# Seven half-size products for one pair of up tiles: a block of the Strassen kind in the MLP of an encoder trunk

## The chip, the cores and the metric

The kernel runs on one core of one Trainium2 chip. The time is the device time of one execution in microseconds. Three runs of the kernel before took 1680.46 to 1681.95 us, the median is 1681.14 us.

The core's engines work side by side and meet through semaphores: TensorE (PE in the profile, PEld for its weight loads) multiplies matrices and writes into PSUM, VectorE (DVE) and ScalarE (ACT) do elementwise work, GpSimd (POOL) and SyncE (SP) here mostly issue DMA transfers.

## The reference: what is computed

Two layers on 512 tokens of width 1024. Each layer has a token part (attention and retention branches, merged and normalised) and a channel part, which is where the change lies:

```python
def conv_glu_ffn(x, w_up, conv_w, conv_b, w_down):
    h = x @ w_up                                    # 512 x 1024 by 1024 x 5632
    hp = jnp.pad(h, ((0, 0), (1, 1), (0, 0)))
    h = hp[:, :-2] * conv_w[0] + hp[:, 1:-1] * conv_w[1] + hp[:, 2:] * conv_w[2] + conv_b
    a, b = jnp.split(h, 2, axis=-1)
    return (jax.nn.gelu(a) * b) @ w_down            # 2816 x 1024
...
ple = jax.nn.sigmoid(x @ w_ple_gate[i]) * (p[i] @ w_ple_proj[i])
x = layer_norm(DEEPNORM_ALPHA * x + ffn + ple, ln2_g[i], ln2_b[i])
```

The convolution runs along the tokens, with a width of three, on each of the 5632 up channels by itself. Everything is float32.

## The kernel before

**Products of split numbers.** Each float32 operand is split into a high part and a low part (`split`, line 169: ACT copies the high part, DVE subtracts to get the low part), and a product is three matmuls, high by high, high by low and low by high (`mm3`, line 395). An instruction name `hi<-raw` in the profile is ACT's cast of a weight, `lo<-raw` is DVE's subtraction for the same weight.

**Weights as a stream.** `Stream` (line 275) holds all weights of the whole program as a list of items in the order in which the products take them. `load` issues the DMA of an item on SP's queue, `prep` splits it into its two halves, and `get` hands it to a product; each `get` first prepares some items ahead (at most `deep`, 5) and loads three more. Plain weights go through a pool of three raw buffers and three pairs of halves (`N_RAW`, `N_W`). For a Strassen-like product, weights are sums of blocks of the matrix: `block_items` (line 187) makes the seven items a, c, t1, t2, d, t3 and t4, where t1, t2 and t4 come from a's raw buffer by adding one more block after another, each by an accumulating DMA on POOL's queue (`add`), and t3 from a second buffer. These two raw buffers (`rawa`, `rawt`) belong to the pool `up`, and so do the halves of the items that are listed as held.

**The pool of units.** `up` is a pool of 30 units (`N_UNIT`, line 29) of 4 KB in each partition. The tiles that live long are taken from it: R, xn, the operands of the down products, sums of x, held weights, own raw buffers. A tile takes a free unit when it is first written and gives it back after its last reader. If none is free, the writing instruction waits.

**Order.** In the MLP the order of the instructions on each of the five queues is pinned to the program's order (`_Ordered.on = set(ORD)`). An instruction that waits holds up all that stands behind it on its engine.

**The MLP's stages.** After the first layer norm, x1 stands transposed in `xt`. The stages are:

- the PLE gate (`pg`, line 1340): seven products of the Strassen kind on halves of x1, with 512 columns each, and between them five plain up tiles. `vg_sums` (line 673) makes the sums of x1 that four of the products take: S, eight units, two for each of t1, t2, d and t3. Behind products c, d, t3 and t4, `ple_gate` multiplies the gate into R and adds xn to it, which frees xn.
- three segments (`SEGS`, line 36) of 3, 4 and 4 pairs of up tiles. Segment 0 has one up tile left beside the five that stand in `pg`. An up tile (`up_tile`, line 1266) is two GEMMs `gemm_t` of 24 matmuls of 128x512, one for each half of the gated unit. ACT scales the middle tap out of PSUM (`ca<-gt,cw`), DVE adds the two side taps, ACT applies GELU to the first half and DVE multiplies. `up_step` (line 1299) splits the result into an operand of the down products: the first tile of a pair gives `a11` (half a unit), the second gives `k2`, and `s_parts` forms the sums `sa` and `sb` of the pair.
- behind each segment, the down products a, c, t1, t2, d, t3 and t4, with 128x512 matmuls over the segment's pairs. N1 halves accumulate in four PSUM banks over all three segments (`w`, `x4`), so the banks that remain are four. In segment 0 the halves of both a's and c's weights are held in units (`HELD[3]`), in segments 1 and 2 those of c's alone. The sums of the last pair are formed after product a.

The matmuls of 128x256 that the change uses exist elsewhere already: `product_t` (line 1078) does the half-size products of the gate blocks in the token part, seven for a block, each with 24 matmuls and x or sums of x as the moving operand.

## Time and profile before

| what | value |
|---|---|
| median of three runs | 1681.14 us (1680.46 to 1681.95) |
| the profiled execution: span from the first to the last instruction | 1679.3 us |
| its own time beside the span | not given by the page; the runs' median is 1.8 us above the span |
| PE busy | 1669.5 us, 99% of the span |
| DVE busy | 1228.2 us, 73% |
| ACT busy | 949.1 us, 57% |
| POOL busy | 189.2 us, 11% |
| DMA | 289.68 MB, mean 172 GB/s |
| granted TensorE clock | 0.999 of full speed |

The profile is of one execution. A group is named by line, engine, operation and the program's tile names, written as out<-in. Most of the MLP's instructions bear line 90, the helper through which the pinned instructions go, so they are told apart by their tiles. The chain of waits is followed back from the last instruction to what released it. A busy PE is not a PE at its peak: matmuls overlap, and what a matmul costs is read from the distance of starts.

### The profile page before, as it was taken

How to read it: one execution, taken by the hardware profiler on the slowest of the kernel's cores; microseconds unless marked ns; L12 is line 12 of the kernel's file. 1: busy time of each engine (PE TensorE's matmuls, PEld its weight loads, DVE VectorE, ACT ScalarE, POOL GpSimd, SP SyncE). 2: the span in 40 equal slices, each digit the busy share in tenths (PEclk: the TensorE clock that was granted, in tenths of full speed). 3: DMA queues.
4: the chain of work that ended last, by engine and by line, in shares of the span. 5: the costliest groups of instructions: out<-in, count | busy, mean ns of one | idle time of the engine just before them, and what ended most of it. 6: DMA issues, size and time to landing. Idle time of an engine off the chain costs nothing.

```text
span 1679.3 us, 22089 instructions
## 1 busy us (share of the span) xinstructions
PE 1669.5 (99%) x8325; PEld 1418.1 (84%) x8325; DVE 1228.2 (73%) x1857; ACT 949.1 (57%) x1418; POOL 189.2 (11%) x216
## 2 busy tenths in 40 slices
PE   9999999999999999999999999999999999999997
PEld 7889988888888888888888899888888888888886
DVE  6756676776787767757876566877688887676678
ACT  6765676853366535335476647668534574353354
POOL 1111111110200100100112011111002010000003
PEclk9999999999999999999999999999999999999999
DMA  8989666666655535535788795667667565265274
GB/s 303 249 234 233 171 149 139 165 173 223 207 135 161 121 112 163 135 111 172 193 231 219 184 245 163 138 144 170 160 241 225 130 171 126 88 181 132 89 212 101
DMA packets 87530, 289.68 MB, mean 172 GB/s; under 512 B 9984, under 2 KB 14592, under 8 KB 87424
## 3 DMA queue, kind: packets, MB, share of 16 engines
q1 hardware_dynamic: 62512, 199.66, 33.7%
q0 software_dynamic: 24912, 88.62, 30.2%
q8 instruction: 65, 1.06, 0.3%
q14 instruction: 41, 0.34, 0.1%
HBM read 269.36 MB, written 17.30 MB: 171 GB/s over the span
## 4 chain that ended last, share of the span: by engine, by line
PE 99%; DVE 1%; ACT 0%; POOL 0%; issue 0%; DVEq 0%; POOLq 0%; ACTq 0%
PE gt L90 31%; PE u L90 13%; PE v L90 7%; PE gt L397 6%; PE gt L398 6%; PE gt L399 6%; PE w L90 4%; PE gn L399 3%; PE gn L397 3%; PE gn L398 3%; PE x L90 1%; PE u L397 1%; PE u L399 1%; PE u L398 1%; PE gn L90 1%; PE na L1023 1%
## 5 line engine op out<-in xcount | busy, mean ns | idle before, releaser
L90 PE MATMUL gt<-x1t,hi 128*128 128x512 f32 x1408 | 433.5, 389 | 0.0
L90 PEld LDWEIGHTS gt<-x1t,hi 128*128 128x128 f32 x1408 | 264.3, 188 | 55.0
L90 PE MATMUL gt<-x1t,lo 128*128 128x512 f32 x704 | 274.1, 389 | 0.1
L90 DVE TENSOR_TENSOR lo<-raw,hi 128x1024 fp32r<-128x1024 f32 (+1 forms) x147 | 175.9, 1206 | 43.5 <-ACT hi L90 43.3
L90 DVE SCALAR_TENSOR_TENSOR ca<-gt,cw,ca 128x511 f32<-128x511 f32 x176 | 131.8, 749 | 78.5 <-ACT ca L90 75.4
L90 ACT CAST hi<-raw 128x1024 fp32r<-128x1024 f32 (+1 forms) x147 | 151.1, 1037 | 33.1 <-PE u L90 13.4
L90 PEld LDWEIGHTS gt<-x1t,lo 128*128 128x128 f32 x704 | 132.2, 188 | 28.1 <-DVE lo L90 1.0
L90 DVE TENSOR_TENSOR lo<-rawa,hi 128x1024 fp32r<-128x1024 f32 x94 | 109.8, 1176 | 49.3 <-ACT hi L90 48.9
L90 ACT ACTIVATE ca<-gt,cw 128x512 f32<-128x512 f32 x88 | 68.5, 779 | 131.7 <-PE gt L90 131.7
L90 ACT CAST hi<-rawa 128x1024 fp32r<-128x1024 f32 x94 | 94.3, 1014 | 39.0 <-DMA rawa<-in_wpack 16.5
L90 POOL DMA_DIRECT2D rawa<-in_wpack x72 | 65.0, 947 | 368.6 <-DVE lo L90 308.0
L397 PE MATMUL gt<-xt,hi 128*128 128x512 f32 x256 | 100.8, 394 | 0.0
L398 PE MATMUL gt<-xt,hi 128*128 128x512 f32 x256 | 99.8, 390 | 0.0
L399 PE MATMUL gt<-xt,lo 128*128 128x512 f32 x256 | 99.7, 389 | 0.0
L170 ACT CAST hi<-raw 128x1024 fp32r<-128x1024 f32 x44 | 45.8, 1050 | 76.2 <-PE gt L398 29.8
L355 ACT CAST hi<-raw 128x1024 fp32r<-128x1024 f32 x48 | 50.4, 1050 | 49.1 <-PE gt L398 41.2
L357 POOL DMA_DIRECT2D lo<-in_wpack x48 | 42.1, 876 | 294.7 <-ACT lo L356 215.4
L90 POOL DMA_DIRECT2D rawt<-in_wpack x20 | 18.8, 1004 | 381.0 <-DMA rawt<-in_wpack 364.8
L171 DVE TENSOR_TENSOR lo<-raw,hi 128x1024 fp32r<-128x1024 f32 x44 | 53.4, 1223 | 10.9 <-ACT hi L170 10.7
L399 PEld LDWEIGHTS gt<-xt,lo 128*128 128x128 f32 x256 | 48.1, 188 | 10.3
L90 PE MATMUL v<-hi,sa 128*128 128x512 f32 x176 | 56.1, 389 | 0.0
L397 PEld LDWEIGHTS gt<-xt,hi 128*128 128x128 f32 x256 | 48.2, 188 | 9.1
(348 smaller groups left out, 4216.9 us busy)
## 6 DMA issues: line engine op xcount, KB each, us to landing
raw<-in_wpack SPq DMA_DIRECT2D x235, 512.0 KB, 3.7
rawa<-in_wpack POOLq DMA_DIRECT2D x84, 512.0 KB, 6.6
lo<-in_wpack POOLq DMA_DIRECT2D x48, 512.0 KB, 5.5
rawa<-in_wpack SPq DMA_DIRECT2D x28, 512.0 KB, 6.8
rawt<-in_wpack SPq DMA_DIRECT2D x28, 512.0 KB, 6.5
rawt<-in_wpack POOLq DMA_DIRECT2D x28, 512.0 KB, 7.2
r_scr<-pp SPq DMA_DIRECT2D x8, 512.0 KB, 10.1
gb<-gb_scr SPq DMA_DIRECT2D x8, 512.0 KB, 5.0
```

Source lines behind the costliest of these rows:

```text
L90: r = f(*a, **k)
L170: nc.scalar.copy(hi, src)
L171: nc.vector.tensor_sub(lo, src, _f(hi))
L355: nc.scalar.copy(hi[:, cs], it.raw[:, cs])
L357: nc.gpsimd.dma_start(lo[:, cs], wpack[l, c][:, o:o + w], accum_op=ALU.add)
L397: nc.tensor.matmul(ps, lh, rh, start=start, stop=False, skip_group_check=more)
L398: nc.tensor.matmul(ps, lh, rl, start=False, stop=False, skip_group_check=more)
L399: nc.tensor.matmul(ps, ll, rh, start=False, stop=stop, skip_group_check=more)
L1023: nc.tensor.matmul(ov[kt], lv, pt[kt // 2][:, sp_, c], start=i == 0 and sp_ == 0, stop=i == 3 and sp_ == 1)
```

## The change

In segments 1 and 2 of each layer, the first pair of up tiles is no longer two plain tiles of two GEMMs each. Its four 128-column stripes of `w_up` are taken as two blocks of 256 columns (one for each half of the gated unit), and both are computed together as one 2x2 block product: `x1` halves by the upper and lower 512 rows, tokens by halves of 256, which gives seven products a, c, t1, t2, d, t3 and t4 of 24 matmuls of 128x256. The moving operands of t1, t2, d and t3 are the sums S that `pg` made for the PLE gate. The order within the segment is written out in `UP_ORDER`, with p for a plain tile: a, c, p, t1, p, t2, d, p, t3, t4, p, p, p.

The block's results are collected in two float32 tiles `uh` (`up_block`): the first product of each output quadrant is copied out of PSUM by ACT, the second is added or subtracted by DVE. The convolution, GELU and the splitting of the pair then work from these tiles and not from PSUM (`up_conv`), in twelve pieces; two pieces stand between the halves of a plain tile and two behind it, for the three plain tiles behind t4, and in the segment's last tile all that are left stand between its halves. A new gate on the stream (`ready`, `APART`) keeps an item whose raw buffer is still being added to from being prepared until four units of work later. The weights of c, d, t1, t2 and t3 of the block are held in units.

```diff
+APART = 4
+UP_HELD = ('c', 'd', 't1', 't2', 't3')
+UP_ORDER = ((), ('0a', '0c', 'p', '0t1', 'p', '0t2', '0d', 'p', '0t3', '0t4', 'p', 'p', 'p'),
+            ('0a', '0c', 'p', '0t1', 'p', '0t2', '0d', 'p', '0t3', '0t4', 'p', 'p', 'p'))
...
+        def up_items(l, s):
+
+            t0, by = 2 * sum(SEGS[:s]), {}
+            for b, t in enumerate(_up_blocks(s)):
+                pos = {(q, 0): (l, UP0 + 2 * t + i, 0, 1024) for i, q in enumerate("acbd")}
+                for it in block_items(pos, {k: up for k in UP_HELD}, VG_EARLY, 1):
+                    it.sent = it.kind in UP_SENT
+                    it.ready = 1 << 30 if it.src is None else 0
+                    by[f"{b}{it.kind}"] = [it]
...
                     if it.nxt is not None:
+                        if it.nxt.ready is not None:
+                            it.nxt.ready = self.work + APART
...
                         it = self.seq[n]
+                        if it.ready is not None and it.ready > self.work:
+                            break
...
-            def up_tile(i):
+            def up_tile(i, between=lambda: None):
                 half = []
                 for ab in range(2):
...
+                    centre(a, ci, ps)
+                    sides(a, ci, ps)
                     half.append(a)
+                    if ab == 0:
+                        between()
...
+            def up_conv(i, p, h):
+
+                G = []
+                for f in range(2):
+                    g = unit_f("cg", (P, 2, 512))
+                    G.append(g)
+                    for ab in range(2):
+                        centre(g[:, ab], ab * NF + i + f, h[ab][:, f])
+                    yield
+                    sides(g[:, 0], i + f, h[0][:, f])
+                    yield
+                    nc.scalar.activation(g[:, 0], g[:, 0], AF.Gelu_apprx_tanh)
+                    sides(g[:, 1], NF + i + f, h[1][:, f])
+                    yield
+                    nc.vector.tensor_mul(g[:, 0], g[:, 0], g[:, 1])
...
+                    nc.scalar.copy(to[:, 0, :], g)
+                    yield
+                    nc.vector.tensor_sub(to[:, 1, :], g, _f(to[:, 0, :]))
+                    yield
+                g1, g2, ta, tb = G[0][:, 0], G[1][:, 0], G[0][:, 1], G[1][:, 1]
+                s_sums(g1, g2, ta, tb)
+                sa[p], sb[p] = unit_r("sa"), unit_r("sb")
+                nc.scalar.copy(sa[p][:, 0, :], ta)
+                nc.scalar.copy(sb[p][:, 0, :], tb)
+                yield
+                nc.vector.tensor_sub(sa[p][:, 1, :], ta, _f(sa[p][:, 0, :]))
+                nc.vector.tensor_sub(sb[p][:, 1, :], tb, _f(sb[p][:, 0, :]))
+                yield
...
+            def up_block(b, kind):
+
+                if kind == "a":
+                    bh[b] = [unit_f("uh", (P, 2, 512)) for _ in range(2)]
+                    bu[b] = bank("u")
+                    product_t(kind, bu[b], True)
+                    nc.scalar.copy(bh[b][0][:, :, H1], v3(bu[b]))
+                elif kind == "c":
+                    w = bank("w")
+                    product_t(kind, w, True)
+                    nc.vector.tensor_add(bh[b][0][:, :, H1], bh[b][0][:, :, H1], v3(w))
...
                         if k == name:
                             r = next(sg)
-                            S = r if isinstance(r, dict) else S
+                            if isinstance(r, dict):
+                                S = r
+                                Sx.clear()
+                                Sx.update(r)
...
+                for k in _up_order(s):
+                    if k == "p":
+                        j = tile - t0
+                        if j == 2 * n - 1:
+                            up_step(j, True, lambda: conv_piece(99))
+                        else:
+                            up_step(j, False, conv_piece)
+                            conv_piece()
+                        residual()
+                        continue
+                    up_block(int(k[0]), k[1:])
+                    conv_piece(1)
+                    if k[1:] == "t4":
+                        b = int(k[0])
+                        late_conv.append(up_conv(_up_blocks(s)[b], b, bh.pop(b)))
```

The host's packing of `w_up` follows the block's layout for these pairs. Nothing else changes; the sizes of all pools, `HELD` and the order of `pg` and of segment 0 are as before.

More of the change, by code (lines that the diff above doesn't have):

```diff
@@ L288, in __init__ @@
                     for s, n in enumerate(SEGS):
-                        for c in range(UP0 + 2 * max(tile, PG.count("up")), UP0 + 2 * (tile + 2 * n)):
-                            plain(c)
-                        tile += 2 * n
+                        self.seq += up_items(l, s)
                         items = down_items(l, s)
@@ L299, in __init__ @@
                 self.xw = None
+                self.work = 0
                 self.deep = DEEP
@@ L1315, in up_step, with a11_of @@
                     s_parts(*sums.pop())
-            a11p = [None]
+            a11p = {}
+            def a11_of(p):
+                if p // 2 not in a11p:
+                    a11p[p // 2] = up.tile([P, 2, 2, 256], F32R, tag="u", name=nm("a11"))
+                a11[p] = a11p[p // 2][:, p % 2]
+                return a11[p]
             def ple_gate(t, c, src, scale):
@@ L1418, in trunk, with conv_piece @@
             for s, n in enumerate(SEGS):
-                for j in range(tile - 2 * sum(SEGS[:s]), 2 * n):
-                    up_step(j, j == 2 * n - 1)
-                    residual()
+                t0, late_conv = 2 * sum(SEGS[:s]), []
+                if s:
+                    a11p.clear()
+                def conv_piece(count=2):
+                    for _ in range(count):
+                        while late_conv and next(late_conv[0], 0) == 0:
+                            late_conv.pop(0)
+                tile += 2 * len(_up_blocks(s))
+                for k in _up_order(s):
+                    if k == "p":
+                        j = tile - t0
+                        if j == 2 * n - 1:
+                            up_step(j, True, lambda: conv_piece(99))
+                        else:
+                            up_step(j, False, conv_piece)
[7 more added lines that the diff above has]
+                        late_conv.append(up_conv(_up_blocks(s)[b], b, bh.pop(b)))
                 fin = s == len(SEGS) - 1
@@ L1693, in _pack @@
     su = _stat(w_up)
-    for i in range(NF):
-        ch += [su[i], su[NF + i]]
+    blocks = [t for s in range(len(SEGS)) for t in _up_blocks(s)]
+    for i in range(0, NF, 2):
+        if i in blocks:
+            w = w_up.reshape(2, 4, P, 2, NF // 2, 256)
+            ch += [w[int(k in "cd"), :, :, int(k in "bd"), i // 2].transpose(1, 0, 2).reshape(P, 1024) for k in "acbd"]
+        else:
+            ch += [su[i], su[NF + i], su[i + 1], su[NF + i + 1]]
     ch += _blocks(w_down)
```

59 lines of the change are left out of this document (47 added, 12 removed).

## The prediction

> **What bounds the kernel now.** I read the page first (engine shares, then the chain that ended last), then the chain in order of time around the MLP, then TensorE's own timeline where half-size products already exist, and last VectorE's (DVE's) timeline at the two places where a "down" stage begins.
>
> ```profile
> span 1679.3 us, 22089 instructions
> ...
> PE 99%; DVE 1%; ACT 0%; POOL 0%; issue 0%; DVEq 0%; POOLq 0%; ACTq 0%
> ```
>
> TensorE (PE) is the chain for 99% of the span. A microsecond of matmul taken away is a microsecond gained, and any gap opened on PE is lost in full. In order of time:
>
> ```profile
> 546.99 10.88 PE gt L90 x48
> 557.87 4.08 PE u L90 x18
> 561.95 4.08 PE w L90 x18
> ...
> 586.43 87.04 PE gt L90 x384
> 673.47 5.44 PE u L90 x24
> ```
>
> These are layer 0's last up tile of segment 0 (48 matmuls), its down products a (u) and c (w), the eight up tiles of segment 1 (16 GEMMs of 24 matmuls without a gap), and the next a product. A 128x512 matmul costs 87.04/384 = 0.2267 us, a GEMM 5.44, a tile 10.88. The span is one profiled execution; the median of the runs, 1681.14, lies 1.8 us above it (launch and end), and I add changes to that median.
>
> **1. The products.** Half-size products exist in the gate blocks. Two consecutive c products, 48 matmuls of 128x256, then a plain GEMM and the next block:
>
> ```profile
> 120.44 0.28 PE L397 MATMUL w<-xt,hi 128*128 128x256 f32 x1
> ...
> 126.08 0.28 PE L399 MATMUL w<-xt,lo 128*128 128x256 f32 x1
> 126.20 0.40 PE L397 MATMUL gt<-xt,hi 128*128 128x512 f32 x1
> ...
> 131.67 0.28 PE L397 MATMUL v<-sh,hi 128*128 128x256 f32 x1
> ```
>
> The durations (0.28, 0.40) overlap, so I go by starts: 126.20 - 120.44 = 5.76 us for 48, that is 0.120 us each and 2.88 per product, more than half of 5.44. Removed per block: two tiles, 4 x 5.44 = 21.76. Added: 7 x 2.88 = 20.16. Gain 1.60 us. A plain GEMM behind a half-size product takes 131.67 - 126.20 = 5.47, 0.03 more; four such places in the block's order make 0.12. Net 1.48 per block; with two segments in two layers 5.9 us. So the stake is small: 0.35% of the time.
>
> [...]
>
> **2. More work for the other engines.** Per block there are three more weights to prepare (seven for four), seven reads of half products (four copies on ACT, three adds on DVE), and four accumulating DMAs on POOL's queue. The convolution, GELU and splits stay the same in number.
>
> ```profile
> 586.40:673.50 87.10, 87.10 (x386) 72.13 (x385) 60.72 (x81) 39.39 (x54) 3.45 (x4) 1.00 0.45 139
> ```
>
> This is segment 1's up stretch: PE, weight load, DVE 60.72, ACT 39.39, POOL 3.45, clock, DMA share 0.45. DVE gains 3 x 1.22 (row `lo<-raw`, 128x1024, in point 3) and 3 x at most 0.69: 66.4 of 85.6 us, 78%. ACT gains three casts and four copies; at a DVE pass's price each that is 6.4, so at most 46. POOL gains four issues at 3.45/4 = 0.9, and the DMA share grows by about a tenth. In the mean all this lies beside PE, so I cost it at nothing. If that cover fails in DVE, each missing microsecond shows on PE at once.
>
> It fails a little at the segment's end. The last tile now has the block's four remaining pieces put between its halves, ahead of the weights of the down stage on DVE's queue. The rows of that place now:
>
> ```profile
> 670.33 1.22 DVE L90 TENSOR_TENSOR lo<-rawa,hi 128x1024 fp32r<-128x1024 f32 x1
> 671.46 2.35 DVE L90 TENSOR_TENSOR lo<-raw,hi 128x1024 fp32r<-128x1024 f32 x2
> ...
> 677.34 0.69 DVE L90 TENSOR_TENSOR k<-ca,k 128x512 fp32r<-128x512 f32 x1 [0.69 <-ACT k L90]
> ...
> 683.42 0.68 DVE L90 TENSOR_TENSOR sb<-tb,sb 128x512 fp32r<-128x512 f32 x1
> ```
>
> 670.33 is a's second weight, 671.46 c's two, 677.34 the last pair's k2. The pieces are one multiply, a wait for ACT's copy, k2's low part, four half-width sums, a wait, sa's and sb's low parts: four full-width passes (0.65 by starts), two waits of 0.69, and four sums of 0.4, 5.5 us together. a's second weight, ready at 671.55, becomes ready at 677.0; PE wants it halfway through product a, at 673.47 + 2.72 = 676.2. That is a stall of 0.8. k2, ready at 678.0, moves by some 5 (0.5 of idle is used up) to 683.0; its first use is 8.84 us after product a's start, 682.3, and 683.1 with the 0.8. So no second stall. I take 0.8 per segment end, with bounds 0 (the idle in these rows absorbs it) and 3 (DVE arrives late as well): 4 x 0.8 = 3.2.
>
> **3. What the change keeps alive.** This decides. The block's t1, t2, d and t3 multiply sums of x1, the eight units S that `vg_sums` makes for the PLE gate. Today each pair of S is last read in its own gate product; the last such matmul is here:
>
> ```profile
> 530.28 0.39 PE L90 MATMUL u<-hi,sl 128*128 128x512 f32 x1
> ```
>
> With the change all eight stay until segment 2's block. The pool `up` has 30 units (`N_UNIT`), unchanged. Where it is fullest, at the end of the PLE gate, the own-buffer loads of segment 0's down stage begin, and 25 us later DVE works through this queue:
>
> ```profile
> 522.32 0.42 SPq L90 DMA_DIRECT2D rawa<-in_wpack  x1
> 522.79 0.42 SPq L90 DMA_DIRECT2D rawt<-in_wpack  x1
> 525.65 0.33 SPq L90 DMA_DIRECT2D rawa<-in_wpack  x1
> 527.75 0.33 SPq L90 DMA_DIRECT2D rawt<-in_wpack  x1
> ```
>
> ```profile
> 549.02 0.69 DVE L90 TENSOR_TENSOR lo<-rawa,hi 128x512 fp32r<-128x512 f32 x1
> 549.97 1.22 DVE L90 TENSOR_TENSOR lo<-raw,hi 128x1024 fp32r<-128x1024 f32 x1 [0.26 <-ACT hi L90]
> 551.88 0.69 DVE L90 TENSOR_TENSOR R<-R,psg 128x512 f32<-128x512 f32 x1 [0.69 <-ACT psg L90]
> 552.61 0.69 DVE L90 SCALAR_TENSOR_TENSOR R<-xn,R 128x512 f32<-128x512 f32 x1
> 553.22 0.68 DVE L90 TENSOR_TENSOR R<-R,psg 128x512 f32<-128x512 f32 x1
> 553.94 0.69 DVE L90 SCALAR_TENSOR_TENSOR R<-xn,R 128x512 f32<-128x512 f32 x1
> 554.55 0.69 DVE L90 TENSOR_TENSOR lo<-raw,hi 128x512 fp32r<-128x512 f32 x1
> 555.15 1.53 DVE L90 SCALAR_TENSOR_TENSOR ca<-gt,cw,ca 128x511 f32<-128x511 f32 x2
> 556.60 1.22 DVE L90 TENSOR_TENSOR lo<-rawa,hi 128x1024 fp32r<-128x1024 f32 x1
> 558.72 1.54 DVE L90 SCALAR_TENSOR_TENSOR ca<-gt,cw,ca 128x511 f32<-128x511 f32 x2 [0.90 <-ACT ca L90]
> 560.66 0.69 DVE L90 TENSOR_TENSOR ca<-ca,ca 128x512 f32<-128x512 f32 x1 [0.41 <-ACT ca L90]
> 562.04 0.69 DVE L90 TENSOR_TENSOR k<-ca,k 128x512 fp32r<-128x512 f32 x1 [0.69 <-ACT k L90]
> ```
>
> I count the units in use when 549.97 (the low half of c's first weight) runs: R 4; xn 2 (tiles 2 and 3, last read at 552.61 and 553.94, behind it); a11 2; k2, sa, sb of two pairs 6; the four own buffers of the SP rows; a's two weights 4; c's first weight 2. That is 24. With S it is 32, and the pool has 30. The order on each engine is pinned, so nothing behind 549.97 can free a unit first. The earliest release is product a's first half: 12 matmuls after 557.87, at 560.6. So 549.97 moves to 560.65 or later, and everything behind it with it. By the starts of the rows: c's first weight 1.14, the four R passes 2.67, c's second weight 0.60, two convolution pairs 1.45 each and t1's first weight 1.14, the multiply 0.69, the wait for ACT and k2's low part 1.38: 10.5 us. k2 of the last pair is ready at 571.2 instead of 562.7. PE wants it in the second half of product c, which starts at 561.95 + 2.72 = 564.7. That is a gap of 6.5 us, the lower bound per layer. It is 7.1 if the row 549.02 waits as well, as its partner on ACT is issued ahead and takes the 30th unit. ACT has its own casts queued behind the same units; DVE is the later of the two. sa and sb follow k2 by about 3.5 us and PE's t1 wants them 4.1 us later, so nothing is added there.
>
> The upper bound takes one more row, the time to landing of SP's loads:
>
> ```profile
> raw<-in_wpack SPq DMA_DIRECT2D x235, 512.0 KB, 3.7
> ```
>
> SP loads c's weight behind the four own buffers. If the last of those waits for the same release, c's data is issued at 560.7 and lands 3.7 later; with a cast of about 1 us and the 10.5 us, k2 is ready at 576, a gap of 11 to 12; a t4 weight that finds no unit adds 2 or so. Bounds per layer 6.5 to 14; I take 8, near the lower, because that one is counted and the rest needs an unlucky order. Two layers: 16.
>
> [...]
>
> In segment 1 the count at 671.46 is 22 for c's first weight and 23 for the second; with S 30 and 31, so the second waits for product a's first half, 676.2. The pieces of point 2 push it there anyway. Segment 2's block has used S up before that point.
>
> **Sum.** Products -5.9, segment ends +3.2, units +16: +13.3. 1681.1 + 13.3 = 1694.4 us.
>
> **Rivals.** (A) Faster: S finds room, because some tile I counted is released sooner than its last reader's row says. Then 1681.1 - 5.9 + 3.2 = 1678.4, or 1675.2 with hidden segment ends. It decides at two units: with 30 in place of 32 there is no wait. For it: before needs 24 here, and the stall rests on my count, not on a row. Against it: every one of the 24 has its last reader in the rows or later. Chance 0.16, half of it within 0.2% (3.4 us, about what a measurement can tell). (B) DVE, not units, is the loss: the pieces come on top of plain tiles at 78% load, DVE arrives some 3 us late at each segment end, and k2 is 3 us late: 4 x 3 - 5.9 = +6, 1687 without any shortage. For it: 677.34 has only 4.3 us of slack today. Against it: half of the block's work falls into stretches with idle DVE. Chance 0.08. (C) The shortage at its upper bound, with loads queued behind it: 2 x 14 + 3.2 - 5.9 = +25, 1706. Chance 0.2. The forecast itself has 0.56, with 1688 (2 x 6.5, no loss at segment ends) to 1701 as its own range.
>
> **How the numbers follow.** Below 1677.8 is half of A, 0.08; within 0.2% is the other half and a little of B, 0.09; the rest is slower, 0.83. The range starts at 1684 and ends at 1708, beyond B, the forecast and C.
>
> **What would show it.** Right: half-size up products at 0.120 us starts; in both layers a gap of 6 to 14 us on PE inside the first down stage (product c, or a and t4 beside it), with DVE idle for some 10 us before it and released by PE; up stretches of segments 1 and 2 at 85.5 us in place of 87.04; gaps of at most a microsecond at their ends. Wrong: PE unbroken from the PLE gate to segment 1 (then A), or gaps only at the ends of segments 1 and 2 (then B). The forecast falls if the units' waits land on SP's prefetches alone, where nothing on PE is due.

## The result and the profile after

| kernel | time | against the kernel before, 95% interval |
|---|---|---|
| before | 1680.8 us (1680.24 to 1681.95) | 1 |
| after | 1767.82 us (1765.72 to 1769.33) | 1.0517 (1.0502 to 1.0532) |

The change makes the kernel 87 us slower, where 13 were predicted. The head of the page of after:

```profile
span 1766.1 us, 22795 instructions
...
PE 1694.5 (96%) x8613; PEld 1441.8 (82%) x8613; DVE 1247.9 (71%) x1881; ACT 967.4 (55%) x1446; POOL 203.8 (12%) x232
```

PE's busy share has gone from 99% to 96%, and the granted clock over the whole span from 0.999 to 0.981. DVE's share is 71%, two points less than before: the share over the span says nothing of what follows.

To find the lost time I took the distance of starts of each two neighbouring matmuls, less the undisturbed 0.2267 or 0.120 us, and added up what is left over by product. Both layers together, core 0:

| where | lost, us |
|---|---|
| segment 0, products c and t1, two layers | 19.9 |
| segments 1 and 2: t3 to t4, and the slow matmuls behind, four times | 22.3 |
| the last two up tiles, four times | 7.6 |
| product a, four times | 30.0 |
| product t2, four times | 11.4 |

That is 91.2; less the 5.9 that the half-size products save, 85.3, and the spans differ by 86.8. So nearly everything is in five places. About 71 of the 91 are gaps, about 20 are matmuls that run slower behind a gap (granted clock 0.50 to 0.65 in the windows under "The clock").

**Segment 0.** PE's timeline (start, duration, engine, line, operation and tiles, count, and the idle time before it with what ended it), and DVE's:

```profile
564.44 0.40 PE L108 MATMUL w<-hi,k 128*128 128x512 f32 x1
571.56 0.79 PE L108 MATMUL w<-hi,k 128*128 128x512 f32 x1 [6.72 <-ACT k L108]
572.15 0.63 PE L108 MATMUL w<-lo,k 128*128 128x512 f32 x1
572.58 1.05 PE L108 MATMUL w<-hi,k 128*128 128x512 f32 x2
```

```profile
548.38 0.69 DVE L108 TENSOR_TENSOR lo<-rawa,hi 128x512 fp32r<-128x512 f32 x1
560.73 1.23 DVE L108 TENSOR_TENSOR lo<-raw,hi 128x1024 fp32r<-128x1024 f32 x1 [11.65 <-ACT hi L108]
...
571.54 0.69 DVE L108 TENSOR_TENSOR k<-ca,k 128x512 fp32r<-128x512 f32 x1 [0.74 <-ACT k L108]
```

```profile
559.64 1.05 ACT L108 CAST hi<-raw 128x1024 fp32r<-128x1024 f32 x1 [11.29 <-PE u L108]
```

DVE stands still for 11.65 us ahead of the low half of c's first weight, which starts at 560.73 (predicted 560.65), and k2's low part comes at 571.54 (predicted 571.2). DVE's row names ACT, whose cast of the same weight waited for a unit as well, 11.29 us, until product a released it. That the two starts agree so closely with the prediction is in part luck: product a starts at 556.95 here and at 557.71 in the kernel before, and the 1.05 us of the cast, which comes behind the same release, were not in the predicted 560.65. PE stands for 7 us in the middle of product c.

**t3 to t4.** PE and DVE around the block's last two products in segment 1 of layer 0:

```profile
642.21 0.28 PE L108 MATMUL u<-sh,hi 128*128 128x256 f32 x1
...
644.97 0.28 PE L108 MATMUL u<-sh,lo 128*128 128x256 f32 x1
648.91 0.50 PE L108 MATMUL u<-x1t,hi 128*128 128x256 f32 x2 [3.67 <-DVE uh L108]
...
650.58 0.63 PE L108 MATMUL u<-x1t,hi 128*128 128x256 f32 x2
651.01 0.41 PE L108 MATMUL u<-x1t,lo 128*128 128x256 f32 x1
```

```profile
643.29 1.53 DVE L108 SCALAR_TENSOR_TENSOR ca<-gt,cw,ca 128x511 f32<-128x511 f32 x2 [2.83 <-ACT ca L108]
644.93 0.69 DVE L108 TENSOR_TENSOR ca<-ca,ca 128x512 f32<-128x512 f32 x1
646.09 0.42 DVE L108 TENSOR_TENSOR a<-ca,a 128x256 fp32r<-128x256 f32 x1 [0.47 <-ACT a L108]
647.03 1.23 DVE L108 TENSOR_TENSOR lo<-raw,hi 128x1024 fp32r<-128x1024 f32 x1 [0.52 <-ACT hi L108]
648.18 0.68 DVE L108 TENSOR_TENSOR uh<-uh,u 128x512 f32<-128x512 f32 x1
654.95 1.23 DVE L108 TENSOR_TENSOR lo<-raw,hi 128x1024 fp32r<-128x1024 f32 x1 [6.09 <-ACT hi L108]
```

t4 accumulates into the bank `u` in which t3's result still stands. t3's last matmul starts at 644.97, but DVE reads it at 648.18 only, behind the tail of the plain tile (side taps, multiply, low part) and a weight. t4 waits 3.7 us for that read and then runs for some microseconds with its matmuls 0.21 us apart (650.58, two of them, to 651.01) in place of 0.120, as t3's 24 were (642.21 to 644.97 for 23).

**Product a.** PE and DVE at the start of segment 1's down stage:

```profile
687.96 0.39 PE L108 MATMUL u<-hi,a 128*128 128x512 f32 x1
...
690.45 0.39 PE L108 MATMUL u<-hi,a 128*128 128x512 f32 x1
694.95 0.80 PE L108 MATMUL u<-hi,a 128*128 128x512 f32 x1 [4.11 <-ACT hi L108]
696.21 0.80 PE L108 MATMUL u<-lo,a 128*128 128x512 f32 x1 [0.46 <-DVE lo L108]
696.80 1.06 PE L108 MATMUL u<-hi,a 128*128 128x512 f32 x2
```

```profile
687.80 1.53 DVE L108 SCALAR_TENSOR_TENSOR ca<-gt,cw,ca 128x511 f32<-128x511 f32 x2
689.25 0.68 DVE L108 TENSOR_TENSOR cg<-cg 128x512 f32<-128x512 f32 x1
690.62 0.69 DVE L108 TENSOR_TENSOR k<-cg,k 128x512 fp32r<-128x512 f32 x1 [0.69 <-ACT k L108]
...
694.07 0.68 DVE L108 TENSOR_TENSOR sb<-cg,sb 128x512 fp32r<-128x512 f32 x1
694.93 1.23 DVE L108 TENSOR_TENSOR lo<-rawa,hi 128x1024 fp32r<-128x1024 f32 x1 [0.17 <-ACT hi L108]
```

The pieces in the last tile (689.25 to 694.07) hold up a's second weight as predicted, for 5.5 us. But DVE arrives late: the side taps of the last tile's first half start at 687.80, 0.16 us before product a. In the kernel before, DVE's row is

```profile
668.88 1.54 DVE L90 SCALAR_TENSOR_TENSOR ca<-gt,cw,ca 128x511 f32<-128x511 f32 x2 [0.29 <-ACT ca L90]
```

and product a's first matmul starts at 673.30, 4.4 us behind it.

**The clock.** Windows of the same trace behind the three gaps, and one undisturbed window (columns: length, then busy time and count of PE, PEld, DVE, ACT and POOL, granted clock, DMA share, GB/s):

```profile
571.56:575.20 3.64, 3.64 (x9) 2.82 (x10) 2.92 (x7) 1.34 (x3) 0.86 (x1) 0.51 0.69 125
649.00:653.20 4.20, 4.20 (x25) 4.20 (x26) 0.00 (x0) 0.00 (x0) 0.00 (x0) 0.65 0.37 125
695.00:701.50 6.50, 6.04 (x14) 4.43 (x15) 5.53 (x6) 3.18 (x5) 0.86 (x1) 0.50 0.55 96
596.00:600.00 4.00, 4.00 (x35) 4.00 (x35) 2.15 (x2) 1.23 (x2) 0.20 (x1) 1.00 0.76 151
```

In the windows of 3.6 to 6.5 us behind these gaps a clock of 0.50 to 0.65 is granted, which by the distance of starts makes 1.4 to 2.6 us more per gap.

### The profile page after: what moved, and what is told of

Its sections match the earlier page's. It is cut to its first block, busy times and chain, and to the rows that moved or that the text cites. A ratio compares the mean times of both kernels' runs of the same rounds, so it can differ in the third digit from the quotient of the medians.

```text
span 1766.1 us, 22795 instructions
## 1 busy us (share of the span) xinstructions
PE 1694.5 (96%) x8613; PEld 1441.8 (82%) x8613; DVE 1247.9 (71%) x1881; ACT 967.4 (55%) x1446; POOL 203.8 (12%) x232
## 5 line engine op out<-in xcount | busy, mean ns | idle before, releaser
L108 PE MATMUL gt<-x1t,hi 128*128 128x512 f32 x1152 | 355.9, 390 | 3.2 <-ACT hi L108 3.2
L108 PEld LDWEIGHTS gt<-x1t,hi 128*128 128x128 f32 x1152 | 215.3, 188 | 48.4 <-ACT hi L108 4.9
L108 PE MATMUL gt<-x1t,lo 128*128 128x512 f32 x576 | 224.8, 390 | 2.2 <-DVE lo L108 2.1
L108 DVE TENSOR_TENSOR lo<-rawa,hi 128x1024 fp32r<-128x1024 f32 x110 | 129.4, 1183 | 60.3 <-ACT hi L108 59.9
L108 DVE SCALAR_TENSOR_TENSOR ca<-gt,cw,ca 128x511 f32<-128x511 f32 x144 | 107.8, 749 | 82.6 <-ACT ca L108 80.1
L108 POOL DMA_DIRECT2D rawa<-in_wpack x84 | 76.2, 946 | 582.0 <-DVE lo L108 538.0
L108 ACT CAST hi<-rawa 128x1024 fp32r<-128x1024 f32 x110 | 111.3, 1020 | 56.4 <-DMA rawa<-in_wpack 28.1
L108 PEld LDWEIGHTS gt<-x1t,lo 128*128 128x128 f32 x576 | 108.2, 188 | 27.3 <-DVE lo L108 4.8
L108 ACT ACTIVATE ca<-gt,cw 128x512 f32<-128x512 f32 x72 | 56.1, 779 | 113.2 <-PE gt L108 113.2
L389 ACT CAST hi<-raw 128x1024 fp32r<-128x1024 f32 x48 | 50.4, 1051 | 49.0 <-PE gt L437 41.2
L438 PEld LDWEIGHTS gt<-xt,lo 128*128 128x128 f32 x256 | 48.1, 188 | 10.3
L436 PEld LDWEIGHTS gt<-xt,hi 128*128 128x128 f32 x256 | 48.2, 188 | 9.0
L437 PEld LDWEIGHTS gt<-xt,hi 128*128 128x128 f32 x256 | 48.2, 188 | 8.9
```

The costliest lines, as they stand in the source:

```text
L108: r = f(*a, **k)
L389: nc.scalar.copy(hi[:, cs], it.raw[:, cs])
L436: nc.tensor.matmul(ps, lh, rh, start=start, stop=False, skip_group_check=more)
L437: nc.tensor.matmul(ps, lh, rl, start=False, stop=False, skip_group_check=more)
L438: nc.tensor.matmul(ps, ll, rh, start=False, stop=stop, skip_group_check=more)
```

## The experiments

Theory after the result: three causes with places of their own. Units: the sums S kept alive, segment 0. Bank: t4 waits for the read of t3. Crowding: DVE has too much to do from t4 to the middle of product a. The rivals stand with each experiment.

### e1: the kernel before, with the sums kept alive

```diff
+            kept_s = {}
             pg()
...
                     up_step(j, j == 2 * n - 1)
                     residual()
+                    if s == 2 and j == 4:
+                        for t in [t for k in ("t1", "t2", "d", "t3") for t in kept_s[k]]:
+                            nc.vector.tensor_copy(small("ks", 1), _f(t[:, 0, :1]))
```

> The kernel before, with nothing of the change but that the eight units S live on: eight DVE copies of one column each (a few hundredths of a us each) read them behind segment 2's fifth up tile. Theory (units): in both layers a gap of 6 to 8 us on PE in product c of segment 0's down stage, as in the changed kernel (564.44 to 571.56), with a slower clock behind it: 1680.8 + 2 x 9.6 = 1700, bounds 1694 to 1706. Rival (the gap needs the block itself, its loads ahead or its held weights): no gap there, 1681 to 1683.

1703.33 us, 1.0134 (1.0119 to 1.0149): 22.8 us slower with no block at all. DVE and PE in segment 0:

```profile
561.13 1.23 DVE L90 TENSOR_TENSOR lo<-raw,hi 128x1024 fp32r<-128x1024 f32 x1 [11.65 <-ACT hi L90]
```

```profile
564.82 0.39 PE L90 MATMUL w<-hi,k 128*128 128x512 f32 x1
571.98 0.80 PE L90 MATMUL w<-hi,k 128*128 128x512 f32 x1 [6.77 <-ACT k L90]
```

The same wait of 11.65 us and the same gap as in after: the units alone do it. Product c loses 9.2 and t1 0.8 in layer 0; 1.1 more goes in t2 of segment 1. (The copies take 0.14 us each, more than the expectation had, but PE loses nothing where they stand.)

### e2: a's weights of segment 0 out of the units

```diff
-HELD = {3: ("a", "c"), 4: ("c",)}
+HELD = {3: ("c",), 4: ("c",)}
```

> The changed kernel, but in segment 0's down stage a's weights go through the three common pairs of halves and not through four units. Theory (units): 28 units in place of 32 where the 30 didn't do, so the gap in product c goes: 1767.8 - 2 x 9.6 = 1748.6, bounds 1745 to 1752, and the four segments with a block stay as they are. Rival (the wait only moves): with three pairs for a's and c's weights something else comes late in the same stage, 1760 to 1770.

1751.11 us, 1.0419 (1.0404 to 1.0435), 16.7 less than after. The gap in product c is gone. Some of it comes back: t1 and t2 of segment 0 lose 1.1 and 2.8 us in layer 0, since a's weights are now prepared later (ACT casts them at 546.93 and 552.77, in after at 540.76 and 547.74). The four segments are as they were.

### e3: t4 in a bank of its own

```diff
                 elif kind == "t3":
                     product_t(kind, bu[b], False)
+                    nc.scalar.copy(bh[b][0][:, :, H2], v3(bu[b]))
                     nc.vector.tensor_sub(bh[b][1][:, :, H2], bh[b][1][:, :, H2], v3(bu[b]))
                 else:
-                    product_t(kind, bu[b], False)
-                    nc.scalar.copy(bh[b][0][:, :, H2], v3(bu[b]))
+                    x = bank("x")
+                    product_t(kind, x, True)
+                    nc.vector.tensor_add(bh[b][0][:, :, H2], bh[b][0][:, :, H2], v3(x))
```

> The changed kernel, but t4 goes into a PSUM bank of its own: ACT copies the bank of t3 out, DVE subtracts it as before, and DVE adds t4's bank (one DVE pass more per block, ACT's copies as many as before). Theory (t4 waits for the read of t3 that stands in DVE's queue behind the plain tile's tail): the gap of 3.8 us ahead of t4 and the slow matmuls behind it go, 4 x 5.2 = 21 less, 1747; if DVE's lateness in the last tile is a consequence of this gap (ACT's copy of t4 comes late and holds up the casts), another 4 x 5 goes with it, 1725 to 1730. Rival (DVE is simply overloaded in the segment): what is won ahead of t4 is lost again at the segment's end, 1760 to 1770.

1743.72 us, 1.0378 (1.0361 to 1.0396), 24.1 less than after: t3 and t4 lose nothing, although DVE has a pass more per block. The second half of my theory fell: product a still loses 7.3 us in the first of the segments and the two up tiles 0.98 and 0.94, so the segment's end isn't a consequence of this gap.

### e4: no pieces in the last tile

```diff
-                def conv_piece(count=2):
+                def conv_piece(count=3):
```

> The changed kernel, but the twelve pieces of the block's convolution stand six and six in the two plain tiles behind t4, so that none stands in the segment's last tile. Theory (the pieces in the last tile hold up a's second weight, c's and k2 on DVE's queue): of the 10 to 14 us that each segment loses in its last GEMMs and in products a and t2, two thirds or more go: 1767.8 - 4 x 8 = 1736, bounds 1725 to 1745. Rival (DVE's work in the three tiles behind t4 is too much wherever it stands): the same lateness moves into the tiles ahead, the time stays within 10 us, 1758 to 1778.

1772.54 us, 1.0548 (1.0533 to 1.0564): 4.7 more, not 32 less. In layer 0's segment 1, product a loses 2.8 in place of 7.7, but the two up tiles ahead lose 1.1 and 5.7 in place of 0.97 and 0.94. The lateness moves with the pieces. Their place ahead of a's second weight isn't the cause by itself.

### e5: e2 and e3 together

```diff
-HELD = {3: ("a", "c"), 4: ("c",)}
+HELD = {3: ("c",), 4: ("c",)}
...
+                    x = bank("x")
+                    product_t(kind, x, True)
```

> The changed kernel with both edits: a's weights of segment 0 in the common pairs, and t4 in a bank of its own. Theory (two separate causes, each in its own stage): the gains add up, 1767.8 - 16.7 - 24.1 = 1727.0, bounds 1724 to 1730, and what is left above 1674.9 (1680.8 less the products' 5.9) are the four segment ends at 11 to 13 us each. Rival (what one edit frees, the other's stage takes): 1735 or more.

1726.66 us, 1.0270 (1.0253 to 1.0287). The two gains add up to within a microsecond, 16.7 + 24.1 = 40.8 against 41.2: two causes, each in its own stage. All that follows is built on this kernel. Its windows from the block's start to t4's end, and from there to a's second weight:

```profile
587.92:640.77 52.85, 52.85 (x313) 47.16 (x312) 32.20 (x40) 22.90 (x31) 3.46 (x4) 1.00 0.49 140
640.77:683.61 42.84, 36.92 (x160) 29.24 (x158) 31.88 (x48) 20.03 (x29) 2.62 (x3) 0.98 0.52 147
```

In the first stretch DVE is busy for 32.20 of 52.85 us, 61%. In the second it has 31.88 us of work, and PE needs three tiles and half a product there, 3 x 10.88 + 2.72 = 35.4 us: 90%. That leaves 3.5 us for pauses, and DVE has 42.84 - 31.88 = 10.96 us of them, most in wait for ACT. Most of what is left of the loss lies at the end of that stretch.

### e6: without the block's side taps

```diff
-                    sides(g[:, 0], i + f, h[0][:, f])
...
-                    sides(g[:, 1], NF + i + f, h[1][:, f])
```

> As e5_both, but the block's two channel pairs get only the middle tap of the convolution: eight DVE passes of 0.73 us per block are left out (the side taps of these channels are not computed). Theory (DVE has too much to do between t4 and the down stage): 5.8 us less work there take back most of the 11.6 us a segment, 1727 - 4 x 8 = 1695, bounds 1685 to 1705. Rival (the waits between ACT and DVE in the pieces cost, not the passes): the pieces wait for each other as before, 1715 to 1727.

1710.78 us, 1.0179 (1.0164 to 1.0194). 5.8 us of DVE work less give 4.0 us per segment, half of what I expected. The time lies between the two ranges: the passes count, but they aren't all.

### e7: four pieces directly behind t4

```diff
                         late_conv.append(up_conv(_up_blocks(s)[b], b, bh.pop(b)))
+                        conv_piece(4)
```

> As e5_both, with the same twelve pieces, but four of them directly behind t4, where DVE is idle for 3.9 us in the trace with t4's own bank (650.9 to 654.8, before the plain tile's first half arrives), then four and four in the next two plain tiles, none in the last one. Theory (order: DVE waits early and is late afterwards, the total would fit): most of the 11.6 us a segment goes, 1727 - 4 x 9 = 1691, bounds 1680 to 1705. Rival (the total is too much for three plain tiles and a product, wherever the pieces stand, as moving them ahead already gained nothing): 1720 to 1735.

1717.55 us, 1.0220 (1.0205 to 1.0235): 9.1 less than e5, a quarter of what I expected, and outside both theories' ranges. Products t1 and t2 now lose 2.7 and 3.6 in the first segment. The window from t4's end to a's second weight, as in e5:

```profile
640.97:679.90 38.93, 36.45 (x158) 28.98 (x157) 31.91 (x48) 20.96 (x30) 2.62 (x3) 1.00 0.52 151
```

DVE has as much work there as in e5, 31.91 us, but 7.02 us of pauses in place of 10.96, and a's second weight is ready 38.9 us behind t4 in place of 42.8. Using one pause of 3.9 us isn't enough.

### e8: six plain weights without DVE

```diff
                     out += [Item("w", (l, UP0 + 2 * t + i, 0, 1024), 1024) for i in range(2)]
+                    for it in out[-2:]:
+                        it.sent = s > 0 and t >= t0 + 2 * SEGS[s] - 3
```

> As e5_both, but the low parts of the six plain weights behind t4 in each of the four segments are made by ACT and an accumulating DMA in place of DVE: six DVE passes of 1.22 us less, 7.3 us a segment, six ACT passes of 1 us and six DMA issues on POOL's queue more; the pieces and their waits stay. Theory (DVE's work is too much): 1727 - 4 x 9 = 1691, bounds 1683 to 1705. Rival (the waits between ACT and DVE in the pieces cost): ACT's casts are then later still, 1720 to 1740.

1748.71 us, 1.0404 (1.0389 to 1.0420), 22 more than e5 and worse than both theories said. PE in the segment's last tile:

```profile
664.49 0.61 PE L108 MATMUL gt<-x1t,hi 128*128 128x512 f32 x2
670.32 0.80 PE L108 MATMUL gt<-x1t,lo 128*128 128x512 f32 x1 [5.22 <-DMA lo<-in_wpack]
```

The low part now arrives by a transfer that ACT's two passes have to come before. ACT makes them at 662.12 and 663.20, behind a cast of a piece for which it waited 2.55 us, and PE stands for 5.22 us.

### e9: no DVE pass at all in the pieces

```diff
-                    sides(g[:, 0], i + f, h[0][:, f])
-                    sides(g[:, 1], NF + i + f, h[1][:, f])
-                    nc.vector.tensor_mul(g[:, 0], g[:, 0], g[:, 1])
-                    nc.vector.tensor_sub(to[:, 1, :], g, _f(to[:, 0, :]))
+                    nc.scalar.copy(to[:, 1, :], g)
...
-                s_sums(g1, g2, ta, tb)
```

> As e5_both, but the block's convolution has no DVE pass at all: side taps, the multiply, the sums and the low parts are left out or made by plain ACT copies (the pair's operands are then wrong), so 10.9 us of DVE passes per block go and ACT gets six copies more. Loads, products, held weights and accumulating DMAs stay as they are. Theory (all that is left of the loss in the four segments is DVE's work crowded behind t4): the four ends cost nothing or little, 1674.9 + 4 in segment 0 = 1679, bounds 1677 to 1688. Rival (late loads or the accumulating DMAs behind the block's have a share of their own): product t2 stays late by 3 to 4 us per segment, 1692 or more.

1698.73 us, 1.0107 (1.0092 to 1.0122): 27.9 less than e5. Product a and the up tiles lose nothing. t1 and t2 together lose 5.7, 3.9, 4.0 and 3.7 in the four segments, as the rival had it. PE and ACT there:

```profile
689.74 0.39 PE L108 MATMUL v<-hi,sa 128*128 128x512 f32 x1
693.00 0.49 PE L108 MATMUL u<-hi,sb 128*128 128x512 f32 x1 [2.87 <-ACT hi L108]
694.26 0.79 PE L108 MATMUL u<-lo,sb 128*128 128x512 f32 x1 [0.77 <-DVE lo L108]
694.85 1.05 PE L108 MATMUL u<-hi,sb 128*128 128x512 f32 x2
```

```profile
691.90 1.05 ACT L108 CAST hi<-rawa 128x1024 fp32r<-128x1024 f32 x1 [4.32 <-DMA rawa<-in_wpack]
```

t2's weight is a's raw buffer with two blocks added, one after the other; PE waits for ACT's cast, and ACT waits for the second accumulating transfer.

### e10 and e11: passes moved to POOL

```diff
-                    nc.vector.tensor_mul(g[:, 0], g[:, 0], g[:, 1])
+                    nc.gpsimd.tensor_tensor(g[:, 0], g[:, 0], g[:, 1], ALU.mult)
...
-                    nc.vector.tensor_sub(to[:, 1, :], g, _f(to[:, 0, :]))
+                sub(a11[p][:, 1, :], g1[:, H1], _f(a11[p][:, 0, :]))
+                sub(k2[p][:, 1, :], g2, _f(k2[p][:, 0, :]))
```

> As e5_both, but of the block's convolution only the eight side taps (5.8 us) stay on DVE; the two multiplies, the sums and the four low parts go to POOL (by the profile's rows 1.27 us for 128x512 and 0.71 for 128x256, twice DVE's; about 12 us per block on an engine that has 3.5 us of issues in the stretch), and ACT's casts of them stand a piece later than what they wait for; two of the eight pieces stand behind t4. Theory (DVE's work behind t4 and the waits between the engines): 5 us less on DVE and fewer waits, better than e6's 1710.8 at the same number of DVE passes less, 1695, bounds 1685 to 1708. Rival (POOL is too slow or disturbs DVE's passes, and its accumulating DMAs come late behind the passes on its pinned queue): 1715 to 1735, with t2 the late product.

For e11 also:

```diff
-HELD = {3: ("c",), 4: ("c",)}
+HELD = {3: ("a",), 4: ("c",)}
```

> As e10_pool_passes, but in segment 0 it is c's weights that go through the common pairs, and a's that stay in units. Theory (a's chain of accumulating DMAs for t1 and t2 was delayed when a's weights went through the pairs; c has no chain): the 2 to 4 us that segment 0 still loses in t1 and t2 in each layer go, 5 us less than e10 in all. Rival (three pairs are too few for either, or the unit shortage comes back in part, as two units fewer are needed at one point only): within 2 us of e10 or above it.

1715.68 us, 1.0206 (1.0188 to 1.0223), and with c's weights in the pairs 1718.35, 1.0227 (1.0210 to 1.0244). The rival's time held: better than e5 by 11, not by 32. The up tiles lose 5.2 to 6.9 us in each segment, t2, which the rival named, 0.7 to 5.2. POOL's timeline in e10, and DVE's:

```profile
657.87 2.87 POOL L108 TENSOR_TENSOR cg<-cg 128x512 f32<-128x512 f32 x2
660.36 1.23 POOL L108 DMA_DIRECT2D rawt<-in_wpack  x1
660.97 2.28 POOL L108 TENSOR_TENSOR cg<-cg,cg 128x256 f32<-128x256 f32 x2
```

```profile
657.02 0.69 DVE L108 TENSOR_TENSOR ca<-ca,ca 128x512 f32<-128x512 f32 x1
658.40 2.90 DVE L108 TENSOR_TENSOR k<-ca,k 128x512 fp32r<-128x512 f32 x1 [0.69 <-ACT k L108]
661.22 1.43 DVE L108 TENSOR_TENSOR ta<-ca,ca 128x256 f32<-128x256 f32 x1
```

DVE's low part of a plain tile's k2 takes 2.90 us in place of 0.69 while POOL multiplies, and the sum behind it 1.43 in place of 0.42. Of what is taken off DVE, 2.21 + 1.01 = 3.22 us come back in these two passes alone.

### e12: e9 with nothing in the last tile

```diff
                         late_conv.append(up_conv(_up_blocks(s)[b], b, bh.pop(b)))
+                        conv_piece(4)
```

> As e9_no_dve_in_pieces, but four of the twelve pieces stand behind t4 and four and four in the next two plain tiles, so that in the last tile no ACT copy stands ahead of the cast of a's second weight. In e9 that cast came at 673.64, the two accumulating DMAs behind a's weights were issued at 671.49 and 676.25 (before: 668.89 and 671.84), and t1 and t2 lost 4 to 6 us in each segment. Theory (a's raw buffers go through a chain cast, accumulate, cast, accumulate that has no slack, so a few us of delay of a's second weight come out at t2): the loss in t1 and t2 goes, 1698.7 - 4 x 4.3 = 1681.5, bounds 1678 to 1687. Rival (t1 and t2 are late for another reason, the loads ahead or DVE's reads): 1694 or more.

1694.14 us, 1.0083 (1.0066 to 1.0100), 4.6 less than e9 where 17 were expected. t1 and t2 lose 4.3, 1.4, 3.8 and 0.8 in the segments. But the edit did only a part of what it was for: four of ACT's copies now stand ahead of a's first weight, and the two accumulating DMAs are issued at 673.60 and 676.18, 1.7 us ahead of product a's start and 0.9 behind it (e9: 2.2 ahead and 2.6 behind; before: 4.4 and 1.5 ahead). So the chain still starts late, and the run doesn't settle whether it has no slack.

### e13: the convolution by halves of the tokens

The side taps of the first 256 tokens stand in the plain tiles behind c and behind d, those of the last 256 directly behind t4; then multiply, casts, sums and low parts in four pieces, none in the last tile.

```diff
+SLOTS = {(0, 0): 1, (0, 1): 1, (2, 0): 1, (2, 1): 1, (3, 0): 1, (3, 1): 1, (4, 0): 1, (4, 1): 1}
...
+                half_centre(0, H1)
+                yield
+                half_sides(0, False)
+                yield
+                half_centre(1, H1)
+                yield
+                half_sides(1, False)
+                yield
+                half_centre(1, H2)
+                half_sides(1, True)
+                half_centre(0, H2)
+                half_sides(0, True)
```

> As e5_both with the whole convolution on DVE, but by halves of the tokens: the side taps of the first 256 tokens are done as soon as those quadrants are finished (four half-width passes of 0.4 us in the plain tile behind c, four in the one behind d), those of the last 256 directly behind t4, and nothing of the block stands in the segment's last tile. Theory (crowding: between t4 and the middle of product a DVE has about 38 us of work for 35 us): 3 us of passes move ahead of t4, 3 into the 3.9 us that DVE idles behind t4, so some 32 us are left for 35; better than e7 (1717.6), 1700, bounds 1688 to 1710. Rival (the amount of DVE work in the segment costs, not where it is): 1713 to 1727.

1698.36 us, 1.0108 (1.0093 to 1.0123): 28.3 less than e5, with every pass still on DVE. Windows of this trace like those of e5, from the block's start to t4's end and from there to a's second weight:

```profile
589.24:642.09 52.85, 52.85 (x313) 47.16 (x312) 34.44 (x47) 24.88 (x35) 3.45 (x4) 1.00 0.50 140
642.09:676.52 34.43, 33.93 (x151) 27.73 (x150) 30.28 (x49) 20.18 (x31) 2.62 (x3) 1.00 0.57 170
```

PE is busy for 33.93 of the second stretch's 34.43 us. Product a loses nothing, the last two up tiles 0.8.

DVE's work in that stretch is hardly less than in e5, 30.28 us in place of 31.88 (the expectation's 38 were too many), and still 86% of the 35.4. What fell is its pauses, from 10.96 to 34.43 - 30.28 = 4.15 us: the wait behind t4 is 1.64 in place of 3.85 us, and three short waits for ACT remain of nine. So the 28 us were not the amount of DVE work in the segment, and only to a small part its amount behind t4; they were pauses in a stretch that has room for few; leaving passes out, as e6 and e9 do, makes room as well. Three things change together here (passes ahead of t4, passes in the pause behind it, fewer handovers between DVE and ACT with none of the block's in the last tile), and no run takes them apart. That the time equals e9's is chance, since the losses lie elsewhere: e9 loses 17.3 us in t1 and t2 of the four segments. In e13 there are left 7.7 us in segment 0, 3.3 in the up tiles and 11.5 in t2; less the products' 5.9 this gives 16.6, and the spans of e13 and before differ by 16.7.

### e14: e13, with c's low parts by DMA

```diff
+            for it in out:
+                it.sent = n == 4 and it.kind == "c"
```

> As e13_halves_early, but the low parts of the down stages' c weights in the four segments are made by ACT and an accumulating DMA (two DVE passes of 1.22 less just ahead of the last pair's k2; c's halves lie in units and are wanted a whole product later). Theory (crowding): 2.3 us less at the tightest place, 4 to 8 us better than e13 in all. Rival (the DMA's landing is too late, or POOL's queue holds a's chain up): t2 or c later, same as e13 or worse.

1718.02 us, 1.0222 (1.0207 to 1.0237), 20 more than e13. The rival held: product c waits for the transfer and loses 8.0 to 8.6 us in each segment.

### e15: a's weights in units where units are free

```diff
             if s == len(SEGS) - 1:
+                held["a"] = up
...
+            if n == 3:
+                next(it for it in out if it.kind == "c").pool = None
```

> As e13_halves_early, with three edits: in segment 0 both of a's weights and c's second lie in units again and only c's first goes through a common pair (30 units where the 30 have to do); in segment 2 a's weights lie in units too, since the sums are given up there; the block's four sums stand one piece later, behind a plain weight that was 0.7 us late. Theory (t2 is late because a's weights, in pairs, are prepared too late for the chain of accumulating DMAs): segment 0 loses 1 in place of 3.8 us a layer, t2 in segment 2 nothing in place of 1 to 3, the plain weights nothing in place of 0.8: 1698.4 - 5.6 - 3.8 - 3.2 = 1686, bounds 1682 to 1692; t2 of segment 1 stays late by 3.9. Rival for segment 0 (one of the 30 is not free in time): the gap in product c comes back, 1705 or more.

1706.03 us, 1.0154 (1.0137 to 1.0171): 7.7 more than e13, not 12 less. Segment 0 came out as expected: it loses 0.7 and 1.0 us in the two layers, so 30 units do where 32 didn't. The rest fell: t1 loses 2.5 to 4.1 in each segment, where e13 lost next to nothing, in segment 1 too, whose only edit is that the block's sums stand a piece later, closer to a's weights. Whether a's weights in units help t2 can't be read from this run, since the later sums hide it.

## Why the prediction was wrong

**The products: right.** 2.88 us per half-size product, and the up stretch of segment 1 takes 687.96 - 595.12 = 92.84 us, of which 7.3 are the losses listed above: 85.5, as predicted. One small thing in the working is not borne out, and nothing hangs on it: what the 1.8 us above the span are ("launch and end") no run shows.

**What the change keeps alive: right in mechanism, place and nearly in size.** The count of 32 for 30 units, the release by product a's first half and the queue behind it came as written (from the waiting weight at 560.73 to k2's low part at 571.54, DVE's rows in after stand in the order of before); e1 shows the cause alone, and e15 that two units fewer are enough. Taken was 8 per layer within 6.5 to 14, measured 9.6 and 10.3. The gap is 6.9 us and 0.75 ahead of it; the rest is the slower clock behind the gap (0.51 over 3.64 us in layer 0), which the sum didn't have.

**"In the mean all this lies beside PE, so I cost it at nothing": the step that failed most.** The mean was about right: over segment 1's up tiles DVE is busy for 63.80 of 86.36 us in e13, 74%, where the prediction had 78%. But that stretch has two parts. While the seven products run, DVE has little to do (61% in e5's window); the whole convolution of the block, 10.9 us of passes (eight side taps, two multiplies, four sums and four low parts), comes behind t4 on top of three plain tiles and the down stage's first weights. There 31.88 us of passes leave 3.5 of 35.4 us for pauses, and DVE has 10.96, since each piece waits for ACT or for the next tile. The prediction divided the work by the whole segment and gave the pauses no place. e13, with nearly the same passes behind t4 and 4.15 us of pauses, saves 28.3 us.

**"0.8 per segment end, bounds 0 and 3": mis-sized by the same error.** The 5.5 us of pieces in the last tile were right. The arrival was not: the sum let DVE arrive as before, and it arrives 4.3 us later. Product a loses 7.1 to 7.7 in place of 0.8, and with the last two up tiles and t2 a segment's end loses 10.3 to 14.6, where the upper bound was 3. Rival B named DVE and this place, but priced it at 3 us late; its kind was right, its price a quarter. e4 shows that the lateness isn't the pieces' place in the last tile, as point 2 had it, but travels with them.

**Not in the sum: the wait of t4 for the read of t3.** I went through the block's order for the 0.03 us of a plain GEMM behind a half-size product, but not for which product accumulates into a bank that is still to be read, and what stands ahead of that read in DVE's queue. e3 puts it at 24.1 us for the four.

**Not in the sum: the clock.** About 20 of the 91 us are matmuls at a slower clock (0.50 to 0.65 in the windows above), most of them behind the gaps of 3.8 to 6.9 us. A gap on PE was priced at its own length.

**Segment 1's second weight of c, and the rivals.** No wait of its own shows at that weight: ACT casts both of c's weights without a pause behind a's second (from 694.80 in after). Rivals A and C fell: S finds no room, and the loads behind the shortage didn't add to it. The forecast's own text said that gaps only at the segments' ends would speak for B; both kinds came, and the larger part was B's.

**What stays open.** In e13 and e12 t2 still loses 1 to 4 us per segment. PE waits there for a weight that goes through two accumulating transfers behind a's second weight, and that weight is prepared later than before. In segment 1 of layer 0, ACT's cast behind the second transfer comes 20.6 us after product a's start in e13 (696.23) and 14.6 in the kernel before (687.91). Of these 6.0 us, 4.3 are the later issue (11.9 us after product a's start in place of 7.6) and 1.7 the time from issue to cast (8.7 in place of 7.0). Why the second is longer, and whether an earlier chain would remove the loss, isn't shown. None of the versions beats the kernel before; the most that the change could give is the products' 5.9 us.

## What to carry to other kernels

Where work is gathered behind the last of several products, count the other engine's work for that stretch alone, up to the next deadline of its queue, and not for the stage. Count its pauses too: e5 and e13 have nearly the same work for 35.4 us, 31.88 and 30.28, and 10.96 and 4.15 us of pauses made the difference. For every product that accumulates into a bank, ask who still has to read that bank and what stands ahead of the read in the reader's pinned queue. And price a gap on PE above its own length: behind the gaps of 3.8 to 6.9 us here the slower clock took 1.4 to 2.6 us more.

## What the runs showed of the hardware that I had not expected

**Gaps cost more than their length.** Behind gaps of 6.9, 3.8 and 4.3 us PE's granted clock is 0.50 to 0.65 over 3.6 to 6.5 us (the windows above), and 128x512 matmuls start 0.43 us apart in place of 0.2267; in e9 a gap of 3.0 and one of 1.0 with a single matmul between them do the same (694.85, two matmuls, to 695.70). Behind most gaps of 0.7 to 1.4 us only one matmul takes 0.34 us, but not behind all: in segment 0 of layer 0 two gaps of 0.86 and 0.76 us with one matmul between them are followed by matmuls 0.43 us apart in e13 (572.56 to 575.12), and two of 1.01 and 0.76 in e9 are not. What decides which gaps bring the slower clock, and why it lasts for 6.5 us behind product a's, stays open.

**Passes of DVE took longer beside POOL's.** In e10 DVE's pass over two operands in SBUF (k2's low part, 658.40) takes 2.90 us in place of 0.69 while POOL runs a tensor_tensor; it ends at 661.30, POOL's two multiplies of 657.87 at 660.74. The side taps, which read PSUM, keep their 1.53 us for two: those that start at 668.88 take 1.52, with POOL's passes of 668.46 and 669.51 beside them. What makes the first longer, the rows don't show.
